# Queries, keys and values of a two-layer mixer in five chunks of 512 columns instead of seven narrower ones

## The chip, the core and the metric

The kernel runs on one core of one Trainium2 chip. The metric is the time of one execution on the device in microseconds (us); a median over runs is given where there are several.

## What is computed

Two layers, one after the other, on a sequence of 256 rows of 1024 columns. Each layer is, cut to what matters:

```python
h = rms_norm(x, norm_g)                        # 256 x 1024
proj = h @ w_in                                # 1024 x 3584
a_q, a_k, a_v, a_g, b_q, b_k, b_v, b_g, m_q, m_g = split(proj)   # 8 x 384, 2 x 256
qa, ka = rope(rms_norm(heads(a_q))), rope(rms_norm(heads(a_k)))  # 6 heads of 64
oa = attention(qa, ka, a_v, causal)
ob = attention(rope(norm(b_q)), rope(norm(b_k)), b_v, three dilated patterns)  # 6 heads
m_k, m_v = split(rms_norm(mem, mem_norm_g) @ w_mem_kv)           # 256 rows of memory
om = attention(rms_norm(heads(m_q)), rms_norm(heads(m_k)), m_v)  # 4 heads, no mask
y = concat([oa * silu(a_g), ob * silu(b_g), om * silu(m_g)])
x = x + y @ w_out
```

All of it is float32.

## The kernel before

**Tiles and engines.** The 256 rows are two tiles `t` of 128; the 1024 columns of the normed input are eight blocks `k` of 128. A projection to n columns sums eight `k`, for both `t`, into two PSUM banks (`project`, L216); gates are projected transposed (`project_t`, L235). Each float32 weight is loaded into `raw` (three buffers, the DMAs issued by SyncE), cast by ScalarE (ACT) into `hi` (L467), and VectorE (DVE) subtracts to get the rest, `lo` (L468); five `hi` and five `lo` can be alive, each 128x1024 or, of a 384-wide chunk, 128x768. The input is split likewise into `xmh` and `xml`. `products` (L146) then issues, for every `k` and `t`, three matmuls: `xmh` with `hi`, `xml` with `hi`, `xmh` with `lo`.

**Chunks.** The columns of the weights come in the order of L410: the memory's keys and values (`mkv`, 512 wide), its queries (`mq`, 256), its gate (`mg`, 256), then for side b and for side a: queries, keys, values (384 each), gate in two parts; then the output projection (`om`, `ob`, `oa`).

**Heads.** `normed` (L270) takes a chunk from PSUM: ACT squares it, DVE sums the squares of each head (`hss`, L262), scales them (`ms`, L155), multiplies the chunk by the tables of the rotation (`t`, L281 and L285), adds (L294) and multiplies by the heads' scales (L295), which GpSimd (POOL) makes with a power (L156). `pair_of_heads` (L302) transposes queries and keys on TensorE (PE), copies them to `qkT`, issues the scores (S), and starts two `head`s (L363): masked add with minimum on DVE (L376; without a mask a plain maximum, `nm`, L369), exponentials on ACT (L371, L378), a reciprocal of the sums on DVE (`rinv`, L382), two scalings on ACT (L384), then transposes of the probabilities `pr` on PE and a copy to `pT` (L395). The values (V) follow, and `y` (L359) is split into `yT` (L593, L594). `pr` has three buffers (`PR_BUFS`).

**What sets the order.** PE's order is written by a planner: `clock` adds the estimated time of each matmul, `spawn` starts a pair or a head after a delay (`D_NORM`, `D_MEM`, `D_SOFTMAX` and others), `poll` lets waiting ones issue between the `k` steps of a projection, `until` holds one back until its turn. The other engines take their instructions in program order as long as `pinning[0]` holds, that is from the start to the end of the memory's queries in layer 0 and for a few steps later; after that a tile scheduler orders them. Each engine's order is fixed when the kernel is built, and an instruction whose input is late holds what stands behind it on its engine. `split(s)` issues casts and subtractions up to `ahead[0]` units ahead of the weights that PE takes. `normed_rows`, `next_mem` and `row_scale` make the normed input, the next layer's memory and the row scales `rmem` of the memory, whose rows `mem_sb` are loaded late (L503).

Of the kernel before, what the change touches and what calls it, by code (L numbers as in the profile page):

```python
# [27 lines left out]
PR_BUFS = 3  # L28
# [39 lines left out]
def hybrid_kernel(ctx: ExitStack, tc: tile.TileContext, x, mem, mem_t, gains, w_in, w_out, w_mem_kv, qk_g, const, out):  # L68
# [26 lines left out]
    mem_sb = cp.tile([P, NT, D], F32, name="mem_sb")  # L95
# [174 lines left out]
    def normed(accs, n, dsts, tables, scale=None):  # L270

        h = n // HD
        half = dict(s=2, d=HD // 2)
        held = []
        for t, acc in enumerate(accs):
            t2, ss = head_squares(acc, n)
            rs = head_scale(ss, n, 1.0 / HD)
            t1 = sp.tile([P, n], F32, tag="t1", name="t1", bufs=2)
            first = tables[0][t][:, None, :].to_broadcast([P, h, HD])
            if scale is None:  # L280
                pin(nc.vector.tensor_tensor(heads(t1), heads(acc), first, op=ALU.mult))  # L281
            else:
                pin(nc.vector.scalar_tensor_tensor(heads(t1), heads(acc), scale, first, op0=ALU.mult, op1=ALU.mult))
            if len(tables) > 1:
                pin(nc.vector.tensor_tensor(t2.rearrange("p (h s d) -> p h s d", **half),  # L285
                                            acc.rearrange("p (h s d) -> p h s d", **half)[:, :, ::-1, :],
                                            tables[1][t].rearrange("p (s d) -> p s d", s=2)[:, None]
                                            .to_broadcast([P, h, 2, HD // 2]), op=ALU.mult))
            held.append((t1, t2, rs))

        def rest():
            for (t1, t2, rs), dst in zip(held, dsts):
                if len(tables) > 1:
                    pin(nc.vector.tensor_tensor(t1, t1, t2, op=ALU.add))  # L294
                pin(nc.vector.tensor_tensor(heads(dst), heads(t1), rs.unsqueeze(2).to_broadcast([P, h, HD]),  # L295
                                            op=ALU.mult))
# [3 lines left out]
    live = dict(pr=0, pT=0, o=0, heads=0, pairs=0, s=0, t=0, v=0)  # L300

    def pair_of_heads(qn, kn, pair, masks, v, gate, ready, finished, alone):  # L302
# [10 lines left out]
        yield from until(lambda: live["s"] == me and live["pr"] + 2 <= PR_BUFS)  # L313
# [3 lines left out]
        live["pr"] += 2  # L317
        scores = [work() for _ in range(2)]
# [8 lines left out]
        for j in range(2):  # L327
            rest = head(2 * me + j, scores[j], spans, masks, pTs, D_SOFTMAX - 1.5 * alone)
            spawn(rest, next(rest))
        yield D_SOFTMAX - 1.5 * alone  # L330
        yield from until(lambda: len(pTs) == 2)
        yield D_PT - alone
# [65 lines left out]

    in_cols = {}
    for i, name in enumerate(["aq", "ak", "av", "ag", "bq", "bk", "bv", "bg"]):  # L400
        in_cols[name] = (i * 384, 384)
    for side in "ab":
        c = in_cols[side + "g"][0]
        in_cols[side + "g0"], in_cols[side + "g1"] = (c, 256), (c + 256, 128)
    in_cols["mq"] = (3072, 256)
    in_cols["mg"] = (3328, 256)
    e_rows = {"om": (6, 2), "ob": (3, 3), "oa": (0, 3)}
    order = []
    for l in range(DEPTH):
        order += [(l, c) for c in ["mkv", "mq", "mg", "bq", "bk", "bv", "bg0", "bg1", "aq", "ak", "av", "ag0", "ag1", "om", "ob", "oa"]]  # L410
    units = []
    for i, (l, c) in enumerate(order):
# [3 lines left out]
        else:  # L416
            n = 512 if c == "mkv" else in_cols[c][1]
# [8 lines left out]
    def loads():  # L426
        while loaded[0] < len(units):
# [4 lines left out]
            if c == "mkv":  # L432
                src = w_mem_kv[l]
            elif c in in_cols:
                src = w_in[l][:, in_cols[c][0]:in_cols[c][0] + n]
            else:
                src = w_out[l][e_rows[c][0] * P:, :]
# [4 lines left out]
            step = 1 if u == 0 else 2 if u == 1 else 4 if u == 2 else nk  # L442
            for b in range(0, nk, step):
                e = b + step
                queue = nc.scalar if u == 0 and b < 3 else nc.sync
                pin(queue.dma_start(raws[u][:, b:e],
                                    src[(a + b) * P:(a + e) * P, :].rearrange("(k p) n -> p k n", p=P)))
# [54 lines left out]
    load(RAW_BUFS + 1)  # L502
    pin(nc.sync.dma_start(mem_sb, mem.rearrange("(t p) c -> p t c", p=P)))  # L503
# [15 lines left out]
    for l in range(DEPTH):  # L519
# [46 lines left out]
        else:  # L566
            mkv, steps = project(mem_xs, weights(), 512)
# [16 lines left out]
        def head_tiles(n, nv):  # L584
            return [sp.tile([P, NT, n], F32, tag=c, name=c, bufs=1) for c in ("qn", "kn")] + [
                sp.tile([P, NT, nv], F32, tag="v", name="v", bufs=2),
                sp.tile([P, n // P, T], F32, tag="gate", name="gate", bufs=2)]
# [8 lines left out]
        def start_heads(pairs, e0, qn, kn, masks, v, gate, ready, delay=D_NORM):  # L596
            for pair in range(pairs):
                spawn(pair_of_heads(qn, kn, pair, masks, v, gate, ready,
                                    lambda y, e=e0 + pair: finished(y, e), e0 + pair == 2), delay + D_PAIR * pair)


        qn, kn, kv, gate = head_tiles(256, 512)
        v = kv[:, :, 256:512]
        ready = dict(gate=1e9)
        mq, steps = project(xs, weights(), 256)
# [134 lines left out]
```

## Time and profile before

| | |
|---|---|
| median of 3 runs | 289.95 us (289.36 to 290.56) |
| the profiled execution | 289.94 us |
| its span in the trace | 288.1 us |
| PE busy | 282.3 us, 1810 groups of instructions |
| DVE busy | 205.9 us |
| ACT busy | 199.0 us |
| POOL busy | 53.4 us |
| DMA, share of the span | q1: 48.7% of 16 engines, 46.22 MB |

The profile comes from one execution; the time beside its span is that execution's own. The chain of waits follows the work that ended last back to the start; the list of waits names what an engine stood still for; the timeline gives each group of instructions with its start, and with the idle time before it and who ended that.

### The profile page before, as it was taken

How to read it: one execution, taken by the hardware profiler on the slowest of the kernel's cores; microseconds unless marked ns; L12 is line 12 of the kernel's file. 1: busy time of each engine (PE TensorE's matmuls, PEld its weight loads, DVE VectorE, ACT ScalarE, POOL GpSimd, SP SyncE). 2: the span in 40 equal slices, each digit the busy share in tenths (PEclk: the TensorE clock that was granted, in tenths of full speed). 3: DMA queues.
4: the chain of work that ended last, by engine and by line, in shares of the span. 5: the costliest groups of instructions: out<-in, count | busy, mean ns of one | idle time of the engine just before them, and what ended most of it. 6: DMA issues, size and time to landing. Idle time of an engine off the chain costs nothing.

```text
span 288.1 us, 4967 instructions
## 1 busy us (share of the span) xinstructions
PE 282.3 (98%) x1810; PEld 250.5 (87%) x1810; DVE 205.9 (71%) x461; ACT 199.0 (69%) x446; POOL 53.4 (19%) x72
## 2 busy tenths in 40 slices
PE   6999999999999999999999999999999999999994
PEld 5799999898989998777788999989898989897773
DVE  1798999794659987754686576979755899655423
ACT  3899678877678779688267554868685778777620
POOL 0103993200003300000020079403000312000000
PEclk9999999999999999999999999999999999999999
DMA  7999675527430656528024918360845443820003
GB/s 246 390 367 369 207 220 161 170 55 273 111 109 17 206 171 262 190 109 290 1 91 168 275 54 236 131 175 9 281 115 154 146 132 96 361 73 0 3 0 146
DMA packets 32793, 47.33 MB, mean 164 GB/s; under 512 B 1280, under 2 KB 27648, under 8 KB 32768
## 3 DMA queue, kind: packets, MB, share of 16 engines
q1 hardware_dynamic: 32336, 46.22, 48.7%
q10 hardware_dynamic: 432, 0.79, 0.9%
q8 instruction: 14, 0.23, 0.3%
q14 instruction: 11, 0.09, 0.1%
HBM read 45.96 MB, written 1.05 MB: 163 GB/s over the span
## 4 chain that ended last, share of the span: by engine, by line
PE 97%; DMA 1%; DVE 0%; SPq 0%; DVEq 0%; issue 0%
PE acc L111 79%; PE wk L114 8%; PE wk L111 5%; PE o L111 5%; DMA memT<-in_mem_t_dram 1%; PE o L114 0%; DVE x_sb L706 0%; SPq L487 0%; DVE whole L533 0%; DVEq L736 0%; DVEq L533 0%
## 5 line engine op out<-in xcount | busy, mean ns | idle before, releaser
L468 DVE TENSOR_TENSOR lo<-raw,hi 128x768 fp32r<-128x768 f32 (+1 forms) x90 | 95.3, 1087 | 20.4 <-ACT hi L467 19.3
L467 ACT CAST hi<-raw 128x768 fp32r<-128x768 f32 (+1 forms) x90 | 82.5, 937 | 26.8 <-PE acc L111 16.9
L111 PE MATMUL acc<-hi,xmh 128*128 128x384 f32 (+2 forms) x252 | 66.6, 346 | 0.0
L111 PE MATMUL acc<-lo,xmh 128*128 128x384 f32 (+2 forms) x252 | 63.7, 335 | 0.0
L111 PE MATMUL acc<-hi,xml 128*128 128x384 f32 (+2 forms) x252 | 63.6, 334 | 0.0
L156 POOL TENSOR_TENSOR hrs<-ms,mhalf 128x6 f32<-128x6 f32 (+1 forms) x24 | 29.9, 1248 | 116.0 <-DVE ms L155 115.7
L111 PEld LDWEIGHTS acc<-hi,xmh 128*128 128x128 f32 x252 | 43.0, 189 | 4.1 <-issue 2.2
L111 PEld LDWEIGHTS acc<-lo,xmh 128*128 128x128 f32 x252 | 45.0, 188 | 1.1
L111 PEld LDWEIGHTS acc<-hi,xml 128*128 128x128 f32 x252 | 44.9, 188 | 1.1
L111 PE MATMUL acc<-hi,yT 128*128 128x512 f32 x128 | 40.9, 401 | 0.0
L111 PE MATMUL acc<-xmh,hi 128*128 128x256 f32 x128 | 29.7, 293 | 0.0
L378 ACT ACTIVATE pr<-pr,nm 128x128 f32<-128x128 f32 (+1 forms) x48 | 21.3, 445 | 12.0 <-DVE nm L376 12.0
L111 PE MATMUL acc<-xmh,lo 128*128 128x256 f32 x128 | 28.4, 283 | 0.0
L111 PE MATMUL acc<-xml,hi 128*128 128x256 f32 x128 | 28.3, 283 | 0.0
L111 PEld LDWEIGHTS acc<-hi,yT 128*128 128x128 f32 x128 | 23.0, 188 | 4.8 <-issue 0.7
L384 ACT ACTIVATE pr<-pr,rinv 128x128 f32<-128x128 f32 (+1 forms) x64 | 25.5, 461 | 0.0
L111 PE MATMUL acc<-lo,yT 128*128 128x512 f32 x64 | 25.1, 391 | 0.0
L111 PEld LDWEIGHTS acc<-xml,hi 128*128 128x128 f32 x128 | 21.0, 191 | 0.0
L111 PEld LDWEIGHTS acc<-xmh,lo 128*128 128x128 f32 x128 | 21.0, 191 | 0.0
L111 PEld LDWEIGHTS acc<-xmh,hi 128*128 128x128 f32 x128 | 20.9, 191 | 0.0
L376 DVE CUSTOM_DVE_ANT_0 pr<-wk,cst 128x128 f32<-128x128 f32 (+1 forms) x48 | 14.3, 353 | 8.6 <-PE wk L111 8.3
L395 ACT COPY pT<-wk 128x384 f32<-128x384 f32 (+1 forms) x32 | 15.2, 508 | 7.2 <-PE wk L114 7.1
(83 smaller groups left out, 354.6 us busy)
## 6 DMA issues: line engine op xcount, KB each, us to landing
raw<-in_w_in_dram SPq DMA_DIRECT2D x24, 768.0 KB, 5.5
raw<-in_w_in_dram SPq DMA_DIRECT2D x7, 1024.0 KB, 6.6
raw<-in_w_out_dram SPq DMA_DIRECT2D x6, 1024.0 KB, 4.9
raw<-in_w_in_dram SPq DMA_DIRECT2D x6, 512.0 KB, 4.1
raw<-in_w_out_dram SPq DMA_DIRECT2D x4, 512.0 KB, 4.2
raw<-in_w_mem_kv_dram SPq DMA_DIRECT2D x2, 1024.0 KB, 5.7
raw<-in_w_mem_kv_dram SPq DMA_DIRECT2D x2, 512.0 KB, 6.7
x_sb<-in_x_dram SPq DMA_DIRECT2D x2, 512.0 KB, 6.4
```

What stands on the lines that cost most here:

```text
L111: pe(nc.tensor.matmul(out, a, b, start=start, stop=stop), us)
L114: pe(nc.tensor.transpose(out, a, ident), 0.109)
L156: pin(nc.gpsimd.tensor_tensor(dst, ms, mhalf[:, :n], op=ALU.pow))
L376: nc.vector.tensor_tensor_reduce(out=pr[:, spans[t]], in0=s[:, spans[t]], in1=masks[t], scale=-1.0, scalar=3e38, op0=ALU.add, op1=ALU.min, ...
L378: nc.scalar.activation(pr[:, spans[t]], pr[:, spans[t]], AF.Exp, scale=-1.0, bias=nm[:, t:t + 1], accum_out=sums[:, t:t + 1])
L384: nc.scalar.activation(pr[:, spans[t]], pr[:, spans[t]], AF.Copy, scale=rinv[:, t:t + 1])
L395: nc.scalar.copy(pT[:, :n], ps[:, :n])
L467: pin(nc.scalar.copy(hi, raw))
L468: pin(nc.vector.tensor_tensor(lo, raw, hi.bitcast(F32), op=ALU.subtract))
```

## The change

The six 384-wide chunks of queries, keys and values and the memory's 256-wide queries become five of 512: `c0` = `mq` and columns 128 to 384 of `bv`; `c1` = `bq` and the first 128 of `bk`; `c2` = the rest of `bk`, the first 128 of `aq`, the first 128 of `bv`; `c3` = the rest of `aq` and 256 of `ak`; `c4` = the rest of `ak` and `av`. Gates, `mkv` and output stay. A chunk that joins several column ranges has a DMA for each. `normed` takes spans of columns with their tables and several destinations. Queries and keys of one side share a tile `qk`, and the pairs start as their columns are complete: b's pair 0 after `c1`, its pairs 1 and 2 after `c2`; a's pairs 0 and 1 after `c3`, its pair 2 after `c4`. The values of `bv` that come with `c0` are copied before `c0`'s norm. The memory's row scales, key norm and gains move from behind the memory's queries into the steps of `c0`; `mem_sb` takes the place of the first weights' buffer. `pr` has four buffers; the memory's pairs start 6.5 instead of 9 planner microseconds after the queries; after a 512-wide norm the delay is 9.5; the delays of the partner, of the scores and of two pairs' softmax change.

```diff
-PR_BUFS = 3
+PR_BUFS = 4
...
-D_NORM, D_MEM, D_QK, D_SOFTMAX, D_PT, D_EVAC = 8, 1, 2.5, 5, 2.5, 4
+D_NORM, D_WIDE, D_MEM, D_QK, D_SOFTMAX, D_PT, D_EVAC = 8, 9.5, 6.5, 2.5, 5, 2.5, 4
...
-D_PARTNER, D_SCORES = 5, 14
+D_BUSY, D_SCORED = 1.5, 4
+D_PARTNER, D_SCORES = 8, 14
...
-    mem_sb = cp.tile([P, NT, D], F32, name="mem_sb")
...
+            for a, b, tables in spans:
+                h = (b - a) // HD
+                first = tables[0][t][:, None, :].to_broadcast([P, h, HD])
...
+                for a, b, dsts in outs:
+                    pin(nc.vector.tensor_tensor(
+                        heads(dsts[t]), heads(t1[:, a:b]),
+                        rs[:, a // HD:b // HD].unsqueeze(2).to_broadcast([P, (b - a) // HD, HD]), op=ALU.mult))
...
-        yield from until(lambda: live["s"] == me and live["pr"] + 2 <= PR_BUFS)
+        yield from until(lambda: live["s"] == me and live["pr"] + 2 <= PR_BUFS and clock[0] >= live["next"])
...
+    for name, pieces in (("c0", (("mq", 0, 256), ("bv", 128, 384))), ("mg", (("mg", 0, 256),)),
+                         ("c1", (("bq", 0, 512),)), ("c2", (("bk", 128, 384), ("aq", 0, 128), ("bv", 0, 128))),
+                         ("bg0", (("bg", 0, 256),)), ("bg1", (("bg", 256, 384),)),
+                         ("c3", (("aq", 128, 640),)), ("c4", (("ak", 256, 768),)),
...
-        order += [(l, c) for c in ["mkv", "mq", "mg", "bq", "bk", "bv", "bg0", "bg1", "aq", "ak", "av", "ag0", "ag1", "om", "ob", "oa"]]
+        order += [(l, c) for c in ["mkv", "c0", "mg", "c1", "c2", "bg0", "bg1", "c3", "c4", "ag0", "ag1", "om", "ob", "oa"]]
...
+    mem_sb = sp.tile([P, NT, D], F32, tag="yT0", name="mem_sb", bufs=1)
     pin(nc.sync.dma_start(mem_sb, mem.rearrange("(t p) c -> p t c", p=P)))
...
         else:
+            ahead[0] = SPLIT_BUFS - 2
             mkv, steps = project(mem_xs, weights(), 512)
...
+            if i == 1 and l == 0:
...
+                r_mem += [row_scale(mem_sb, t, "rmem", mem_junk) for t in range(NT)]
+                sums = [head_squares(k, 256)[1] for k in keys]
...
             if i == 3 and l == 0:
-                mem_junk = sp.tile([P, D], F32, tag="v", name="mem_junk", bufs=2)
-                r_mem.append(row_scale(mem_sb, 0, "rmem", mem_junk))
...
-                split(at[1] + t + 3)
...
+        for t, acc in enumerate(accs):
+            pin(nc.scalar.copy(v_b[:, t, 128:384], acc[:, 256:512]))
...
-        start_heads(2, 6, qn, kn, None, v, gate, ready, D_NORM + D_MEM)
+        start_heads(range(2), 6, qn, kn, None, v, gate, ready, D_MEM)
...
-            for i, dst in ((0, qn), (1, kn)):
-                accs = run(project(xs, weights(), 384))
...
+        accs = run(project(xs, weights(), 512))
+        normed(accs, 512, [span(0, 384, 2), span(384, 512, 3)], [(0, 512, by_tile(qk, 0, 512))])()
+        start_heads(range(1), 3, qn, kn, masks, v, gate, ready, D_WIDE)
+        accs = run(project(xs, weights(), 512))
+        normed([acc[:, 0:384] for acc in accs], 384, [span(0, 256, 3), span(256, 384, 0)],
+               [(0, 256, by_tile(qk, 512, 768)), (256, 384, by_tile(qk_a, 0, 128))])()
...
+        start_heads(range(1, 3), 3, qn, kn, masks, v, gate, ready)
```

Two places show how the order moves. The first is DVE in layer 0 around the memory's gate, whose two `lo` are `lo_268` and `lo_305` in before. Before:

```order
L468 TENSOR_TENSOR lo_268<-raw_118,hi_267 128x1024
L155 TENSOR_SCALAR ms_301<-ss_298 128x1
L468 TENSOR_TENSOR lo_305<-raw_118,hi_304 128x1024
L262 TENSOR_REDUCE hss_334<-sq_332 128x4
L155 TENSOR_SCALAR ms_337<-hss_334 128x4
```

After, where `lo_347` and `lo_363` are the gate's, `lo_321` is the last of `c0`, and the rows of `v_260` are the memory's keys:

```order
L262 TENSOR_REDUCE hss_306<-sq_304 128x4
L642 TENSOR_SCALAR r2_308<-rmem_290 128x1
L155 TENSOR_SCALAR ms_311<-hss_302,r2_308 128x4
L642 TENSOR_SCALAR r2_314<-rmem_296 128x1
L155 TENSOR_SCALAR ms_317<-hss_306,r2_314 128x4
L480 TENSOR_TENSOR lo_321<-raw_117,hi_320 128x1024
L649 SCALAR_TENSOR_TENSOR t1_338<-v_260,rmem_290,gB_94 128x256
L652 TENSOR_TENSOR v_260<-t1_338,hrs_310 128x256
L649 SCALAR_TENSOR_TENSOR t1_341<-v_260,rmem_296,gB_94 128x256
L652 TENSOR_TENSOR v_260<-t1_341,hrs_316 128x256
L480 TENSOR_TENSOR lo_347<-raw_267,hi_346 128x1024
L480 TENSOR_TENSOR lo_363<-raw_267,hi_362 128x1024
```

The gate's first `lo` moved from ahead of the memory's key norm to behind it.

The second place is b's pair 0 in layer 0: DVE from the last work ahead of its two softmaxes (`pr_909` and `pr_920` in before) to the first reciprocal. Before:

```order
L468 TENSOR_TENSOR lo_864<-raw_832,hi_863 128x768
L468 TENSOR_TENSOR lo_939<-raw_832,hi_938 128x768
L376 ISA pr_909,nm_910<-wk_898,cst_94 128x128
L376 ISA nm_910 128x1
L376 ISA pr_909,nm_910<-wk_898,cst_94 128x256
L376 ISA nm_910 128x1
L376 ISA pr_920,nm_921<-wk_899,cst_94 128x128
L376 ISA nm_921 128x1
L376 ISA pr_920,nm_921<-wk_899,cst_94 128x256
L376 ISA nm_921 128x1
L468 TENSOR_TENSOR lo_980<-raw_861,hi_979 128x768
L382 RECIPROCAL rinv_916<-sums_911 128x2
```

After, where the rows of `qk` are the last of `c2`'s norm:

```order
L301 TENSOR_TENSOR qk_498<-t1_802,hrs_798 128x128
L384 ISA pr_846,nm_847<-wk_835,cst_93 128x128
L384 ISA nm_847 128x1
L384 ISA pr_846,nm_847<-wk_835,cst_93 128x256
L384 ISA nm_847 128x1
L384 ISA pr_857,nm_858<-wk_836,cst_93 128x128
L384 ISA nm_858 128x1
L384 ISA pr_857,nm_858<-wk_836,cst_93 128x256
L384 ISA nm_858 128x1
L367 SCALAR_TENSOR_TENSOR y_880<-o_841,gate_261 128x256
L480 TENSOR_TENSOR lo_922<-raw_817,hi_921 128x1024
L390 RECIPROCAL rinv_853<-sums_848 128x2
```

The masked adds stand behind a norm instead of behind subtractions, and `y` of the memory's second pair now stands between them and the reciprocal.

PE at the same place, from the scores of b's pair 0. Before, the transposes of `pr` come 45 gate matmuls and one group of transposes later:

```order
L111 MATMUL acc<-xmh,lo 128x256 x2
L111 MATMUL wk<-qkT 128x128 x2
L111 MATMUL wk<-qkT 128x256 x2
L111 MATMUL o<-pT,v 64x256 x4
L114 MATMUL wk<-ident,qn 128x128
```

After, the rows just ahead of the transposes of `pr`, which also come 45 gate matmuls behind the values:

```order
L111 MATMUL acc<-xmh,hi 128x256
L111 MATMUL acc<-xml,hi 128x256
L111 MATMUL acc<-xmh,lo 128x256
L114 MATMUL wk<-ident,qk 128x128 x4
L114 MATMUL wk<-ident,pr 128x128 x3
```

The queries' and keys' transposes moved from right behind the values to right ahead of the transposes of `pr`; the distance from scores to these stayed.

## Rows read from the trace of the kernel before

**Rows 1.** The page: engines' busy time; the last chain's share by engine

```profile
PE 282.3 (98%) x1810; PEld 250.5 (87%) x1810; DVE 205.9 (71%) x461; ACT 199.0 (69%) x446; POOL 53.4 (19%) x72
...
PE 97%; DMA 1%; DVE 0%; SPq 0%; DVEq 0%; issue 0%
```

**Rows 2.** The list of waits of PE: us in total, times, longest

```profile
PE acc L111 <- DVE whole L533: 1.1, 1, 1.1
PE warm L121 <- DVE mhalf L84: 1.0, 1, 1.0
```

**Rows 3.** Timeline of PE: start, us, engine, line, operation, tiles, count

```profile
12.72 1.07 PE L111 MATMUL acc<-hi,xml 128*128 128x512 f32 x4
13.63 1.07 PE L111 MATMUL acc<-lo,xmh 128*128 128x512 f32 x4
...
19.02 0.40 PE L111 MATMUL acc<-hi,xmh 128*128 128x256 f32 x2
...
30.92 0.51 PE L111 MATMUL acc<-hi,xml 128*128 128x384 f32 x2
...
35.43 0.51 PE L111 MATMUL acc<-lo,xmh 128*128 128x384 f32 x2
```

**Rows 4.** The chain of waits, 30 to 80 us: start, us, what

```profile
39.97 1.06 PE wk L111 x8
41.03 6.46 PE acc L111 x36
...
65.89 0.86 PE wk L111 x8
66.75 1.01 PE o L111 x8
67.77 0.59 PE wk L114 x4
68.35 5.39 PE acc L111 x45
73.74 0.33 PE wk L114 x3
```

**Rows 5.** Timeline of ACT, layer 0, the memory's rows and the memory's squares

```profile
23.07 1.06 ACT L161 ACTIVATE mem_junk<-mem_sb 128x1024 f32<-128x1024 f32 x1 [0.40 <-DMA mem_sb<-in_mem_dram]
24.04 0.18 ACT L161 ACTIVATION_READ_ACCUMULATOR mem_junk<-mem_sb 128x1 f32 x1
...
25.06 0.65 ACT L260 ACTIVATE sq<-acc 128x256 f32<-128x256 f32 x2
```

**Rows 6.** Timeline of DVE: the memory's key norm, and two 1024-wide subtractions

```profile
28.11 0.73 DVE L262 TENSOR_REDUCE hss<-sq 128x4 f32<-128x256 f32 x2
28.76 0.20 DVE L624 TENSOR_SCALAR r<-rmem 128x1 f32<-128x1 f32 x1
...
32.36 0.47 DVE L632 SCALAR_TENSOR_TENSOR t<-v,rmem,gB 128x256 f32<-128x256 f32 x1
...
33.67 0.55 DVE L635 TENSOR_TENSOR kn<-t,hrs 128x256 f32<-128x256 f32 x1
...
155.03 2.36 DVE L468 TENSOR_TENSOR lo<-raw,hi 128x1024 fp32r<-128x1024 f32 x2 [0.63 <-ACT hi L467]
```

**Rows 7.** Timeline of ACT: copies, exponentials and scalings of the memory's pairs

```profile
47.97 1.07 ACT L395 COPY pT<-wk 128x512 f32<-128x512 f32 x2
...
51.24 0.47 ACT L371 ACTIVATE pr<-wk,nm 128x256 f32<-128x256 f32 x1 [2.19 <-DVE nm L369]
...
52.60 0.91 ACT L384 ACTIVATE pr<-pr,rinv 128x256 f32<-128x256 f32 x2
```

**Rows 8.** Timeline of DVE: maxima, norm of 384 columns, first masked add

```profile
50.51 1.29 DVE L369 TENSOR_REDUCE nm<-wk 128x2 f32<-128x512 f32 x2
...
57.31 1.02 DVE L294 TENSOR_TENSOR t<-t,sq 128x384 f32<-128x384 f32 x2
...
66.78 0.29 DVE L376 CUSTOM_DVE_ANT_0 pr<-wk,cst 128x128 f32<-128x128 f32 x1 [2.04 <-PE wk L111]
```

More of the change, by code (lines that the diff above doesn't have):

```diff
@@ L297, in normed, with pair_of_heads @@
         return rest
     pending = {}
-    live = dict(pr=0, pT=0, o=0, heads=0, pairs=0, s=0, t=0, v=0)
-    def pair_of_heads(qn, kn, pair, masks, v, gate, ready, finished, alone):
+    live = dict(next=0, pr=0, pT=0, o=0, heads=0, pairs=0, s=0, t=0, v=0)
+    def pair_of_heads(qn, kn, pair, masks, v, gate, ready, finished, alone, busy):
         ps = work()
@@ L317, in pair_of_heads @@
         live["pr"] += 2
+        live["next"] = clock[0] + D_SCORED
         scores = [work() for _ in range(2)]
@@ L416, in hybrid_kernel @@
         else:
-            n = 512 if c == "mkv" else in_cols[c][1]
+            n = 512 if c == "mkv" else sum(hi - lo for lo, hi in in_cols[c])
             nk = 8 if n <= 256 else 4
@@ new lines, in hybrid_kernel @@
+            if i == 1 and l == 0:
+                mem_junk = sp.tile([P, D], F32, tag="tab", name="mem_junk", bufs=1)
+                r_mem += [row_scale(mem_sb, t, "rmem", mem_junk) for t in range(NT)]
+                sums = [head_squares(k, 256)[1] for k in keys]
+                scales = []
+                for t in range(NT):
+                    r2 = sp.tile([P, 1], F32, tag="r2", name="r2", bufs=2)
+                    pin(nc.vector.tensor_scalar(r2, r_mem[t], r_mem[t], 1.0 / HD, op0=ALU.mult, op1=ALU.mult))
+                    scales.append(head_scale(sums[t], 256, r2))
@@ new lines, in hybrid_kernel @@
+            if i == 3 and l == 0:
+                pin(nc.sync.dma_start(cst, const))
+                load_gains(0, 4)
+                for t in range(NT):
+                    t1 = sp.tile([P, 256], F32, tag="t1", name="t1", bufs=2)
+                    pin(nc.vector.scalar_tensor_tensor(heads(t1), heads(keys[t]), r_mem[t],
+                                                       gB[:, l, 5][:, None, :].to_broadcast([P, 4, HD]),
+                                                       op0=ALU.mult, op1=ALU.mult))
+                    pin(nc.vector.tensor_tensor(heads(kn[:, t]), heads(t1),
+                                                scales[t].unsqueeze(2).to_broadcast([P, 4, HD]), op=ALU.mult))
@@ L642, in hybrid_kernel, with span @@
         tab = prepare_tables(l)
+        def span(a, b, kind):
+            return a, b, [[tab[:, kind, c, t] for t in range(NT)] for c in range(2)]
         gates(run(project_t(xs, weights(), 256)), gate)
@@ new lines, in hybrid_kernel @@
+        for t, acc in enumerate(accs):
+            nc.scalar.copy(v[:, t, 0:128], acc[:, 384:512])
+        start_heads(range(1, 3), 3, qn, kn, masks, v, gate, ready)
+        ready["v"] = clock[0] + D_EVAC
+        gates(run(project_t(xs, weights(), 256)), gate[:, 0:2])
+        gates(run(project_t(xs, weights(), 128)), gate[:, 2:3])
+        masks = [cst[:, C_CAUSAL + 128:C_CAUSAL + 256], cst[:, C_CAUSAL:C_CAUSAL + 256]]
+        if l + 1 < DEPTH:
+            mem_xs = xm_tiles()
+            spawn(next_mem(mem_xs, gT[:, 24 + 8 * l:32 + 8 * l]), D_FIRST_MEM)
@@ new lines, in hybrid_kernel @@
+        (v, gate), qk = head_tiles(384, 384), qk_a
+        qn, kn = qk[:, :, 0:384], qk[:, :, 384:768]
+        ready = dict(v=1e9)
+        accs = run(project(xs, weights(), 512))
+        normed(accs, 512, [span(0, 256, 0), span(256, 512, 1)], [(0, 512, by_tile(qk, 128, 640))])()
+        start_heads(range(2), 0, qn, kn, masks, v, gate, ready, D_WIDE)
+        accs = run(project(xs, weights(), 512))
+        normed([acc[:, 0:128] for acc in accs], 128, [span(0, 128, 1)], [(0, 128, by_tile(qk, 640, 768))])()
@@ L671, in hybrid_kernel @@
+        for t, acc in enumerate(accs):
+            nc.scalar.copy(v[:, t], acc[:, 128:512])
+        start_heads(range(2, 3), 0, qn, kn, masks, v, gate, ready)
+        ready["v"] = clock[0] + D_EVAC
+        gates(run(project_t(xs, weights(), 256)), gate[:, 0:2])
+        gates(run(project_t(xs, weights(), 128)), gate[:, 2:3])
         whole_banks = [(t, c, 512) for t in range(NT) for c in (0, 512)]
```

133 lines of the change are left out of this document (51 added, 82 removed), and 1 row of the table in_cols.

## The prediction

> **What bounds the kernel now.** I read the page first, then the chain of waits, then PE's list of waits, then the timelines of the stages that change. PE is busy 282.3 us of a span of 288.1 us, and the chain that ended last is PE for 97% [rows 1]. PE stands still only twice, in the first microseconds [rows 2]: after that it never waits for anyone. So there are two ways to move the time: give PE fewer or cheaper instructions, or make it wait where it does not wait now. The other engines' busy shares, about 70%, say nothing on the second; only the order at each place does. A row's us of DVE or ACT runs about 0.09 beyond the start of the next instruction (1.06 listed, 0.97 from start to start [rows 5]); I take it off in chains.
>
> All sums are made against the profiled execution, 289.94 us, of which 1.84 lie around the span; the median of the runs, 289.95, is the same number. A difference of 0.5%, about 1.45 us, is about what a measurement of this kernel can tell from no change.
>
> **Fewer matmuls: a gain of 2.5.** From start to start, four matmuls of 512 columns take 0.91, which is 0.2275 for one; 26 of 384 take 4.51, 0.1735 for one [rows 3]; 45 of 256 take 5.39, 0.120 for one [rows 4]. At the granted clock of the higher level, 2.4 GHz, the columns alone would be 0.2133, 0.160 and 0.1067: each matmul has 13 to 14 ns on top. A layer's seven chunks had 6 x 48 + 48 = 336 matmuls, five have 240, with the same 2560 columns per k, t and product. That is 192 fewer in two layers. By the pitches a layer falls from 6 x 48 x 0.1735 + 48 x 0.120 = 55.7 to 240 x 0.2275 = 54.6, 2.2 in all; by 13.4 ns each it is 2.6. PE's trains of matmuls are broken eight times more (66 against 58), at most 0.015 each. I take 2.5, between 2.1 and 2.6. All of it lies on the path, since PE is the path.
>
> The Trainium skill ("TensorE: Matmul & The Clock Gate", section "Wait — 56ns, not 53.3ns?") puts the fixed cost of a warm matmul at about 2.5 ns. By it 192 fewer would give 0.5 and not 2.5. The rows speak against it, with five times that, in this form of matmul.
>
> **The memory's gate in layer 0: a loss of 0.9.** The row scales and key norm of the memory now stand ahead of the gate's first `lo` on DVE. PE starts `c0` where it started the queries, at 19.02 [rows 3], takes 48 x 0.227 = 10.9 for it, and wants that `lo` after four matmuls of the gate, at 30.4. The helpers: the memory's rows land at 23.07 [rows 5]; two squares with their sums read out, 1.06 each, to 25.2; two squares of 256, 0.28 each [rows 5], to 25.8; the second sum over heads 0.32 and the hand-over, to 26.3; four small instructions at 0.2 [rows 6], to 27.1; the last `lo` of `c0`, 1.13 (half of 2.36 less the overlap [rows 6]), to 28.25; the key norm's four instructions at 0.38 and 0.46, 1.7 in all [rows 6], to 30.0; the gate's `lo`, 1.2, to 31.2. PE waits 0.8 to 1.0; I take 0.9, with 0.4 and 1.5 as ends, since POOL's powers and the hand-overs can each be a few tenths off. In layer 1 the gate's `lo` is ahead of the key norm, and nothing is late.
>
> `mem_sb` in the slot of the first weights adds a wait on SP for their release; the queue behind it holds the gains and the next weights. Those first weights are the first four k of `mkv`, which PE has left by 12.7 [rows 3], and the rows land ten microseconds later; I cost it at nothing. Would the load start a microsecond later, the chain above would grow by that microsecond.
>
> **Pair 0 of side b: a loss of 2.4 in each layer.** This is the largest term. Let Z be the end of the first memory pair's scores. PE's order to the scores of pair 0 is: 72 matmuls of 512 (rest of `c1`, all of `c2`) 16.3; the second memory pair's scores 1.06 and 0.21 by which the train behind them is longer (36 x 0.1735 = 6.25 against 6.46 [rows 4]); three groups of four transposes at 0.44 and one of eight at 0.88 (0.11 a transpose [rows 4]); a pair's values 1.22 with the same 0.21; twelve gate matmuls 1.44. Sum: Z + 22.5. The masked scores end at Z + 23.3. From there to the transposes of `pr` it takes as long as in before, 73.74 - 66.75 = 7.0 [rows 4]: PE wants `pr` at Z + 30.3.
>
> The helpers, in their order: the maximum and what is left of a subtraction ahead of it, Z + 1.5 (a maximum 0.6 [rows 8]). ACT then has eight exponentials at 0.46, eight scalings at 0.41, a cast of 0.97 and two copies at 0.49 [rows 5, 7], 8.9 in all, and only then squares `c1`, 0.6: DVE starts `c1`'s norm at Z + 11.0. An operation of 256 columns takes 0.32 [rows 6] and of 384 0.465 [rows 8], so 128 take 0.20 and 512 take 0.60 by the same slope. Per row tile the norm is a sum 0.60, two tables of 384 and 128 columns each 0.67, a small one of 0.1, an add 0.60 and a scaling 0.60, twice, 6.4: Z + 17.4. Five subtractions at 1.13, `y` and its rest at 0.34 each: Z + 23.8. `c2`'s norm: sum 0.465, tables of 256 and 128 at 0.52 twice, 0.1, add 0.465, scalings 0.52, twice, 5.1: Z + 28.9. Only now come the masked adds, two of 128 and two of 256, 1.1: Z + 30.0. `y` of the second memory pair 0.34, a subtraction 1.13, the reciprocal 0.2: Z + 31.6. Two scalings on ACT 0.8: Z + 32.4. PE waits 2.1, and 0.35 more at the second head, whose reciprocal stands behind another subtraction: 2.4. PE's and DVE's orders are alike here in both layers, so 4.8.
>
> In before DVE stood idle for 2.04 ahead of the same masked add and started it as soon as the scores were there [rows 8]; the change uses up that slack and some more. No row shows this stretch itself, so both ends: 1.4 if the first maximum is unobstructed (0.9 sooner) and a few joints are shorter; 3.4 if one more subtraction of 1.1 or the narrow pieces of the norms cost more than the slope. As nothing else can be gained there, the end below 1.4 is no wait, a rival.
>
> **Parts at nothing.** The fourth buffer of `pr` lets scores go sooner, not softmax; its cover is the same DVE work. The memory's pairs start after 6.5 instead of 9: the queries' norm ends about 36.1 by the chain of the gate continued, PE comes to their transposes at about 37.4, after its wait; if that cover is gone, it costs the difference one for one. The value copies ahead of `c0`'s norm, two of ACT at about 0.3, lie in the same 1.3. The norms have 14 more small DVE instructions a layer at some 0.06; the widths are the same, and they are inside the terms above. Four casts and subtractions fewer per layer, each wider, leave DVE 0.5 less to do. More DMAs of the same bytes cost SP some issues; the raw buffers they fill are wanted later than PE's time through a chunk. Side a has the same shape but fewer helpers' tasks in front, with 1.5 to spare at least.
>
> **Sum.** 289.94 - 2.5 + 0.9 + 4.8 = 293.1. With both ends of the three terms, 290.7 to 296.1; several ends together are unlikely, so I take 291.0 to 295.4 for this case.
>
> **Rivals.** (1) *The helpers are in time.* If the reciprocal of pair 0 is ready by Z + 29.5, PE never waits there. For it: the chain has some thirty joints, each from a row elsewhere, and 2.1 of 31.6 is 7%. Against it: DVE's list ahead of the masked adds is solid work. The time is 287.4, or 288.3 with the gate's wait. (2) *The waits are half as long*, 2 to 3 in all: 288.7 to 291.0. That is a chain one microsecond shorter in each layer. (3) *The fixed cost of a matmul is small*: the matmuls give 0.4 and the waits stay, 289.94 - 0.4 + 5.7 = 295.2; rows 3 speak against it. (4) *One more wait*, for the second pair of b, whose margin is about 0.4, or for the cast of the last `k` of `c0`, some 0.3: over 295.4.
>
> **Chances.** Forecast 53%, rival 1 20%, rival 2 20%, rival 3 2%, rival 4 5%. The bounds of 0.5% are 288.5 and 291.4. Faster: 20%, rival 1. The same: rival 2 and 3% at the lower edge of the forecast, 23%. Slower: 57%. The range goes from 287.4 to 295.4; about one in ten lies below, where rival 1's gain is larger than its sum, and one in twenty above. The forecast's own range is 291.0 to 295.4.
>
> **What would show it.** Right: matmuls of 512 at 0.227 throughout the five chunks; PE idle once at the gate of the memory in layer 0, released by DVE's `lo`; PE idle twice in each layer ahead of three transposes of `pr`, about 2.1 and 0.35, released by ACT's scaling, which waited for DVE's reciprocal; DVE without a pause from `c1`'s sum over heads to that reciprocal. Wrong: DVE idle ahead of pair 0's masked adds, as in before; a pause of PE at the transposes of queries and keys; a pitch of 512 columns over 0.23.

## The result, and the profile after

The changed kernel takes 296.78 us (median of 4 runs, 295.50 to 297.42) against 290.25 us for the kernel before, measured beside it: a ratio of 1.0228, 95% interval 1.0203 to 1.0253. The sign was forecast, the size was not: 6.5 us more instead of 3.2, and outside the range of 287.4 to 295.4. The profiled execution took 297.31 us, its span is 295.2 us, 7.1 more than before.

The page of the changed kernel, its busy line and its last chain:

```profile
PE 284.7 (96%) x1618; PEld 229.5 (78%) x1618; DVE 206.0 (70%) x477; ACT 198.9 (67%) x438; POOL 55.4 (19%) x72
...
PE 85%; ACT 6%; DMA 5%; DVE 2%; SPq 1%; issue 0%; DVEq 0%; ACTq 0%
```

Against [rows 1], PE has 192 matmuls fewer and is yet busy longer, and the chain leaves PE for 15% of the span. The list of waits of PE (us in total, times, longest) has three entries that [rows 2] did not have:

```profile
PE wk L114 <- ACT pr L392: 3.6, 2, 1.8
PE acc L111 <- DVE lo L480: 1.1, 1, 1.1
PE warm L121 <- DVE mhalf L85: 1.0, 1, 1.0
PE acc L111 <- DVE whole L546: 0.5, 1, 0.5
PE wk L114 <- DVE xn L522: 0.2, 1, 0.2
```

The timeline of PE shows the first two, at the memory's gate in layer 0 and ahead of the transposes of `pr` of side b's pair 0:

```profile
30.56 0.40 PE L111 MATMUL acc<-xml,hi 128*128 128x256 f32 x2
32.09 0.50 PE L111 MATMUL acc<-xmh,lo 128*128 128x256 f32 x2 [1.13 <-DVE lo L480]
...
75.14 0.60 PE L114 MATMUL wk<-ident,qk 128*128 128x128 f32 x4
77.54 0.84 PE L114 MATMUL wk<-ident,pr 128*128 128x128 f32 x3 [1.80 <-ACT pr L392]
...
218.48 0.84 PE L114 MATMUL wk<-ident,pr 128*128 128x128 f32 x3 [1.80 <-ACT pr L392]
```

And DVE and ACT at the second place, in layer 0: the end of `c2`'s norm, the first masked add, the subtraction ahead of the reciprocal, the reciprocal, the scaling:

```profile
73.06 1.15 DVE L301 TENSOR_TENSOR qk<-t,hrs 128x256 f32<-128x256 f32 x4
74.14 0.28 DVE L384 CUSTOM_DVE_ANT_0 pr<-wk,cst 128x128 f32<-128x128 f32 x1
...
75.58 1.21 DVE L480 TENSOR_TENSOR lo<-raw,hi 128x1024 fp32r<-128x1024 f32 x1
76.71 0.15 DVE L390 RECIPROCAL rinv<-sums 128x2 f32<-128x2 f32 x1
...
77.09 0.80 ACT L392 ACTIVATE pr<-pr,rinv 128x128 f32<-128x128 f32 x2
```

The masked adds start right behind the norm, without a pause; the same add had 2.04 of idle time ahead of it in [rows 8]. The scores themselves were done at 68.6.

What nobody had forecast is behind the second pause. The granted clock of TensorE in three stretches of the changed kernel (the stretch, its length, busy time of PE, PEld, DVE, ACT, POOL, then PEclk, share of DMA, GB/s): around the pause of layer 0, around that of layer 1, and the 2.7 us behind the latter.

```profile
75.50:80.50 5.00, 3.13 (x25) 2.51 (x24) 3.54 (x8) 5.00 (x18) 0.00 (x0) 1.00 0.28 78
216.50:221.50 5.00, 3.13 (x19) 2.57 (x18) 3.33 (x7) 4.77 (x16) 0.00 (x0) 0.88 0.33 92
220.50:223.20 2.70, 2.70 (x14) 2.70 (x14) 0.00 (x0) 1.36 (x4) 0.00 (x0) 0.50 1.02 355
```

After the same 1.80 of pause, layer 0 goes on at 2.4 GHz; layer 1 does so at first (its matmuls are 0.12 apart from 219.40 to 219.87) and then falls to 1.2 GHz: the gate's matmuls there are 0.21 apart (220.70 to 220.92 in the timeline) instead of 0.12, and the stretch from the gate to `c3` is 16.06 in layer 1 against 14.69 in layer 0, 1.4 more.

Where the 7.1 of the span went, by the starts of the stages in the two timelines (a plus is time lost):

| place | us |
|---|---|
| start to `c0` (18.96 against 19.02) | -0.1 |
| last cast of `c0` late (`c0` takes 11.37; 48 matmuls at 0.229 with their breaks are 10.99) | +0.4 |
| gate of the memory, layer 0 (7.13 against 5.76) | +1.4 |
| pair 0 of b, pause and the steps around it, 2 x 2.4 | +4.8 |
| lower clock behind it, layer 1 | +1.4 |
| end of the span behind the last matmul | +0.2 |
| the rest: matmuls and small places | -1.0 |

### The profile page after: what moved, and what is told of

Same layout as the page of the kernel before. It is cut to its first block, busy times and chain, and to the rows that moved or that the text cites. A ratio compares the mean times of both kernels' runs of the same rounds, so it can differ in the third digit from the quotient of the medians.

```text
span 295.2 us, 4600 instructions
## 1 busy us (share of the span) xinstructions
PE 284.7 (96%) x1618; PEld 229.5 (78%) x1618; DVE 206.0 (70%) x477; ACT 198.9 (67%) x438; POOL 55.4 (19%) x72
## 3 DMA queue, kind: packets, MB, share of 16 engines
HBM read 45.96 MB, written 1.05 MB: 159 GB/s over the span
## 4 chain that ended last, share of the span: by engine, by line
PE 85%; ACT 6%; DMA 5%; DVE 2%; SPq 1%; issue 0%; DVEq 0%; ACTq 0%
PE acc L111 68%; PE wk L114 7%; PE wk L111 5%; PE o L111 5%; DMA raw<-in_w_in_dram 3%; ACT hi L479 2%; DMA memT<-in_mem_t_dram 2%; ACT pr L386 1%; DVE lo L480 1%; ACT xmh L183 1%; ACT mem_junk L161 1%; ACT pr L392 0%; ACT v L633 0%; SPq L457 0%; DVE v L652 0%
## 5 line engine op out<-in xcount | busy, mean ns | idle before, releaser
L480 DVE TENSOR_TENSOR lo<-raw,hi 128x1024 fp32r<-128x1024 f32 x78 | 94.5, 1227 | 27.5 <-ACT hi L479 27.2
L479 ACT CAST hi<-raw 128x1024 fp32r<-128x1024 f32 x78 | 81.0, 1052 | 36.1 <-PE acc L111 32.3
L111 PE MATMUL acc<-hi,xmh 128*128 128x512 f32 x188 | 61.4, 411 | 0.0
L111 PE MATMUL acc<-hi,xml 128*128 128x512 f32 x188 | 57.7, 392 | 0.0
L111 PE MATMUL acc<-lo,xmh 128*128 128x512 f32 x188 | 57.6, 391 | 0.0
L156 POOL TENSOR_TENSOR hrs<-ms,mhalf 128x4 f32<-128x4 f32 (+3 forms) x24 | 29.9, 1252 | 134.9 <-DVE ms L155 134.1
L111 PEld LDWEIGHTS acc<-lo,xmh 128*128 128x128 f32 x188 | 35.2, 188 | 8.1 <-DVE lo L480 0.3
L111 PEld LDWEIGHTS acc<-hi,xml 128*128 128x128 f32 x188 | 35.3, 188 | 7.9
L111 PEld LDWEIGHTS acc<-hi,xmh 128*128 128x128 f32 x188 | 32.7, 190 | 7.3 <-issue 2.2
L386 ACT ACTIVATE pr<-pr,nm 128x128 f32<-128x128 f32 (+1 forms) x48 | 21.3, 445 | 11.4 <-DVE nm L384 11.2
L111 PE MATMUL acc<-xml,hi 128*128 128x256 f32 x128 | 28.7, 286 | 0.0
L114 PE MATMUL wk<-ident,pr 128*128 128x128 f32 x104 | 17.5, 280 | 3.7 <-ACT pr L392 3.6
```

Of the source, the lines that this page charges most:

```text
L111: pe(nc.tensor.matmul(out, a, b, start=start, stop=stop), us)
L114: pe(nc.tensor.transpose(out, a, ident), 0.109)
L156: pin(nc.gpsimd.tensor_tensor(dst, ms, mhalf[:, :n], op=ALU.pow))
L386: nc.scalar.activation(pr[:, spans[t]], pr[:, spans[t]], AF.Exp, scale=-1.0, bias=nm[:, t:t + 1], accum_out=sums[:, t:t + 1])
L479: pin(nc.scalar.copy(hi, raw))
L480: pin(nc.vector.tensor_tensor(lo, raw, hi.bitcast(F32), op=ALU.subtract))
```

## The experiments

The theory was that DVE's order makes the waits: key norm ahead of the gate's subtraction, `c2`'s norm ahead of the masked adds. The rivals were that the data are late in any order, that a removed wait comes back at the next user, and that the lower clock and the spread between executions have other causes. All edits are to the changed kernel unless said otherwise.

**e_gate: the key norm two steps later.**

```diff
+            if i == 5 and l == 0:
                 for t in range(NT):
                     t1 = sp.tile([P, 256], F32, tag="t1", name="t1", bufs=2)
```

> The changed kernel with one edit: in layer 0 the memory's key norm stands two steps of c0 later, behind the gate's first subtraction on DVE. The scheduler also sets the reciprocal of side b's pair 0 in layer 0 ahead of a subtraction. Theory (DVE's order makes both waits): PE's wait of 1.13 at the gate is gone, the wait ahead of the transposes of pr in layer 0 falls by one subtraction, from 1.80 to about 0.7, layer 1 stays at 1.80; 296.8 - 1.4 - 1.1 = 294.3. Rival (the memory's data are late for any order, PE waits as long for the next user): no more than 0.3 gained at the gate, 295.5 or more.

297.39 us (295.96 to 298.49), ratio 1.0242 (1.0202 to 1.0282): nothing gained in the median. Yet its trace (296.40) has the wait at the gate gone and that of pair 0 in layer 0 too, where 0.7 had been expected to stay; only layer 1's is left. Its list of waits, first and fourth row:

```profile
PE wk L114 <- ACT pr L392: 1.8, 1, 1.8
...
PE wk L111 <- ACT pr L379: 0.3, 1, 0.3
```

Two things took it back in this execution. `c1` and `c2` take 29.79 instead of 28.80: PE, now 1.4 earlier, comes to the memory's second scores before ACT has freed their buffer. And the first eight matmuls took 6.29 instead of 3.86, of which more below. In the two longest executions (298.37 and 298.49) the mean granted clock is 0.988 and 0.987, in the two others 0.993 and 0.994: it was low for about twice as long there, at a place that no trace shows. So the theory holds for both waits, and the rival holds for most of the gain.

**e_first: the masked adds ahead of `c2`'s norm**, in both layers.

```diff
-        normed([acc[:, 0:384] for acc in accs], 384, ...
...
-        start_heads(range(1, 3), 3, qn, kn, masks, v, gate, ready)
+        def second_norm(..., D=2.4 if True else 0):
+            normed(...)
...
+            start_heads(range(1, 3), 3, qn, kn, masks, v, gate, ready, D_NORM - D)
...
+            spawn(second_norm(), 2.4)
```

> The changed kernel with one edit: c2's norm and the pairs that hang on it start 2.4 planner microseconds into the gate, so that the masked adds of side b's pair 0 stand ahead of that norm on DVE, in both layers. Theory (c2's norm ahead of the masked adds is the cause, and the lower clock follows from the pause): both waits of 1.80 with the 0.6 around each go, and the half clock behind the second too; 296.8 - 4.8 - 1.4 = 290.6, mean clock 1.0. Rival 1 (work is conserved: the norm is late instead and PE waits for the transposes of queries and keys): 294 or more, with a new wait released by qk's scaling. Rival 2 (the clock falls for another reason): waits gone, clock still 0.994, 292.

291.34 us (290.61 to 291.62, 10 runs), ratio 1.0034 (1.0019 to 1.0049). 5.4 of the 6.5 are gone, 0.7 less than expected. Of its waits only the start's and the gate's are left:

```profile
PE acc L111 <- DVE lo L480: 1.1, 1, 1.1
...
PE acc L111 <- DVE whole L546: 0.5, 1, 0.5
```

On DVE the masked adds now follow `c2`'s first sum, 1.6 after PE's scores started, and the reciprocal is there five microseconds earlier than PE wants `pr` (76.10):

```profile
69.85 0.27 DVE L384 CUSTOM_DVE_ANT_0 pr<-wk,cst 128x128 f32<-128x128 f32 x1
...
71.18 0.17 DVE L390 RECIPROCAL rinv<-sums 128x2 f32<-128x2 f32 x1
```

On PE the edit also moves the queries' and keys' transposes behind those of `pr`; PE asks for `pr` 7.9 behind the start of the scores, in the changed kernel 7.8, so this is not what saves the wait. The clock is 1.00 in both layers, and its mean is 0.999 or 1.0 in all ten executions. The norm, which ends 1.4 later, makes nobody wait: the slack was on its side all the time.

**e_first_l1: the same edit in layer 1 alone.**

```diff
-        spawn(second_norm(), 2.4)
+        if l == 1:
+            spawn(second_norm(), 2.4)
+        else:
+            next(second_norm(), None)
```

These lines are against e_first.

> The changed kernel with the masked adds first in layer 1 alone; layer 0 keeps its waits at the gate and at pair 0. Theory: layer 1 gains its 2.4 and the 1.45 at the lower clock, 296.8 - 3.9 = 292.9 with clock 1.0. Rival (the lower clock is not from the pause in layer 1): 294.4, clock below 1.0 after one of layer 0's waits.

293.69 us (293.25 to 294.73), ratio 1.0126 (1.0108 to 1.0145). Its trace (293.47, span 291.3) is 3.9 shorter than the changed kernel's, as expected: 2.4 of waiting and 1.4 of clock belong to layer 1. The medians lie 3.1 apart, since two of the changed kernel's four executions had no fall of the clock (see after_b). Layer 0 keeps its pause of 1.80 and its clock, as the stretch of 75.5 to 80.5 shows:

```profile
75.50:80.50 5.00, 3.13 (x25) 2.50 (x24) 3.48 (x8) 5.00 (x19) 0.00 (x0) 1.00 0.29 89
```

**e_late: PE asks for pair 0's `pr` later**, and DVE still takes `c2`'s norm ahead of the masked adds.

```diff
-    ..., e0 + pair in (5, 7)), delay + D_PAIR * i)
+    ..., (e0 + pair in (5, 7)) + 2 * (e0 + pair == 3)), delay + D_PAIR * i)
```

The number counts units of `D_BUSY`, 1.5.

> The changed kernel with one edit: the transposes of pr of side b's pair 0 are issued 3 planner microseconds later, PE doing other matmuls meanwhile; the DVE's order of norm and softmax stays. Theory (PE only asks too early): the waits of 1.80 are gone in both layers, and the low clock with them, 290.6 to 291.5. Rival (what stands behind pr is then late in turn, values and the next pair's buffers): a new wait of 1 to 2 for a later step of the pairs, 293 or more.

298.69 us (298.03 to 300.26), ratio 1.0297 (1.0262 to 1.0333). The waits of 1.80 are gone, but now the gates and the end of the pairs are late, and PE waits for them eight times, most of it in the output projection:

```profile
PE acc L111 <- DVE gate L596: 2.5, 4, 0.9
PE acc L111 <- ACT yT L610: 2.3, 4, 1.0
```

The rival holds: the pairs are a chain of turns, and what one loses, the last ones pay.

**e_both, and again as e_both_b: both edits of order.**

> Both edits together. Theory: no wait of PE over 0.3 after the start, 296.8 - 1.4 - 4.8 - 1.4 = 289.2, that is 1.0 below before: of the 1.6 that the matmuls' pitch by the trace of after is worth (288 x 0.1736 + 48 x 0.1197 - 240 x 0.229 = 0.78 a layer), 0.5 is lost at the last cast of c0 and other small places. Rival (the five chunks cost something else beside the waits, such as more breaks): 290.5 or more. By the prediction's term of 2.5 for the matmuls it would be 288.2.

> The kernel with both edits once more. Its runs had 290.8 to 294.3 without a wait of PE in the trace of a 291.0 run. Theory (it has another pause in its longer runs, from a load or a helper that is late by chance): the trace shows at 292 or more a wait that the first trace lacks. Rival (only the first matmuls' clock): no wait, the first eight longer by the difference.

292.03 us (290.76 to 294.28, 10 runs), ratio 1.0067 (1.0040 to 1.0095): no better than e_first, 2.8 more than expected, so the rival holds, and up to 295.06 in e_both_b. In the first trace (290.95) PE waits for nobody after the start, but the memory's second scores, a group of eight, take 1.88 in the timeline instead of some 1.1:

```profile
47.40 1.88 PE L111 MATMUL wk<-qkT 64*128 64x256 f32 x8
```

In the second trace (295.06) the same scores stand for 3.12, a wait that the first lacks, as expected. The timelines of PE, ACT and DVE there:

```profile
50.85 1.13 PE L111 MATMUL wk<-qkT 64*128 64x256 f32 x6 [3.12 <-ACT pr L379]
...
46.84 1.04 ACT L479 CAST hi<-raw 128x1024 fp32r<-128x1024 f32 x1 [4.50 <-DMA raw<-in_w_in_dram]
...
47.92 1.23 DVE L480 TENSOR_TENSOR lo<-raw,hi 128x1024 fp32r<-128x1024 f32 x1 [3.32 <-ACT hi L479]
49.06 1.28 DVE L377 TENSOR_REDUCE nm<-wk 128x2 f32<-128x512 f32 x2
```

They are read from the bottom: the maximum of the first scores stands behind a subtraction, that behind a cast, and the cast waits for a load of `c2`, which comes in three pieces; the last landed at 46.74 instead of the first trace's 44.04. A late piece of a load holds, through the orders of ACT and DVE, a softmax that has nothing to do with it. The clock is at 0.57 from 51.5 to 55.5 behind this pause too:

```profile
51.50:55.50 4.00, 4.00 (x15) 2.99 (x13) 2.65 (x5) 4.00 (x14) 0.00 (x0) 0.57 0.00 0
```

**e_piece: `c2` from one range of columns**, otherwise e_both. It computes `bk`'s rest and 256 columns of `bv` in place of `aq`'s and `bv`'s first 128.

```diff
-("c2", (("bk", 128, 384), ("aq", 0, 128), ("bv", 0, 128)))
+("c2", (("bk", 128, 640),))
```

> Both edits, and c2 reads 512 neighbouring columns of the weights in one DMA for each half instead of three; so it computes bk's rest and 256 columns of bv in place of aq's and bv's first 128, and the result is not the reference's. The orders of PE, DVE and ACT are those of both edits alone. Theory (the pieces make the load late): the load of c2's second half lands within 4.5 of its issue in every run, the times lie within 1 of each other around 290.8, no wait at the memory's second scores over 0.3. Rival (the load's lateness has nothing to do with its pieces): the spread stays, 290.8 to 295.

291.16 us (290.61 to 291.52, 12 runs), ratio 1.0020 (1.0001 to 1.0039). The spread is 0.9, where e_both has 3.5 in 10 runs and more with e_both_b, and e_mem8 (below, loads in three pieces) 2.7 in 12: with PE's, DVE's and ACT's order unchanged, the pieces are the likely cause of the long executions, though only one trace shows a late one. Two parts of the expectation failed: the load took 5.0 from issue to landing in its trace, not 4.5, and the wait at the memory's second scores stays, 0.36.

**e_scored, e_warm: e_both with the memory's second scores later; and, in e_warm, two more matmuls on blanks at the start.**

```diff
-        live["next"] = clock[0] + D_SCORED
+        live["next"] = clock[0] + D_SCORED + (masks is None)
...
-WARM = 7
+WARM = 9
```

> Both edits (key norm later, masked adds first) and a third: the scores of the memory's second pair one planner microsecond later, since with the gate's wait gone PE stood 0.29 at them for ACT's exponentials and their group took 2.0 instead of 1.4. Theory: that 0.75 in layer 0 comes back, matmul work from the first cast weights to the end is 274.4 (275.1 with both edits), and the median is 0.7 below that of both edits, 291.3. Rival (the buffer of the scores was not the cause): the first scores' successor waits as long, 292.0.

> The same with nine instead of seven matmuls on blanks at the start, which fill the 0.9 that PE stands still before its first weights. Theory (the spread between executions of the changed kernels is the moment at which PE's clock reaches the higher level, with 1 to 6 of the first eight matmuls at 0.853 instead of 0.429): all eight at 0.429, PE reaches the first cast weights at about 8.2 to 8.7, and the median falls by 1 to 2 against e_scored, to 289.5. Rival (the moment has nothing to do with the pause): same spread, no change.

292.34 us (292.06 to 292.55) and 291.85 us (291.81 to 292.64), ratios 1.0075 (1.0062 to 1.0087) and 1.0067 (1.0053 to 1.0080). The scores no longer wait, the transposes of the probabilities do instead (also 0.78 in layer 1):

```profile
49.70 0.66 PE L114 MATMUL wk<-ident,pr 128*128 128x128 f32 x4 [0.50 <-ACT pr L379]
...
51.91 0.66 PE L114 MATMUL wk<-ident,pr 128*128 128x128 f32 x4 [0.18 <-ACT pT L403]
```

So it is ACT's exponentials, not the buffer of the scores, that are behind there, and the 0.7 expected did not come. e_warm has the same waits but one; its 0.5 less is a wait of 1.05 for a copy of values that its trace lacks, not the start: the first cast weights come at 8.38 there and at 8.20 in e_scored. Its theory fails.

**before_warm: ten matmuls on blanks in the kernel before.**

```diff
-WARM = 7
+WARM = 10
```

> The kernel before with ten instead of seven matmuls on blanks, which fill its pause of 1.57. Its first eight already run at 0.429 from the first. Theory: nothing to gain, 290.0 within 0.2. Rival (the pause costs in some executions): up to 0.5 less and a smaller spread.

290.13 us, ratio 0.9999 (0.9990 to 1.0008). Nothing, as expected.

**e_mem8: e_both with the memory's pairs 1.5 later.**

```diff
-D_NORM, D_WIDE, D_MEM, ... = 8, 9.5, 6.5, ...
+D_NORM, D_WIDE, D_MEM, ... = 8, 9.5, 8, ...
```

> Both edits, and the memory's pairs start 8 instead of 6.5 planner microseconds after c0; loads in three pieces as in the changed kernel. Theory (the early pairs put the memory's maxima behind a subtraction whose load is late): with 1.5 more the second scores wait for nobody in most executions, 290.2 with a spread under 1.5. Rival (the pairs' work is then late for what follows, c1's norm and pair 0): new waits of PE behind it, 291 or more.

291.90 us (290.98 to 293.68), ratio 1.0048 (1.0025 to 1.0070): the rival holds. The second scores wait no more; the transposes behind them do, in its profiled execution for 1.00:

```profile
54.09 0.66 PE L114 MATMUL wk<-ident,pr 128*128 128x128 f32 x4 [1.00 <-ACT pr L379]
```

**e_pr3: three buffers of probabilities.**

```diff
-PR_BUFS = 4
+PR_BUFS = 3
```

> The changed kernel with three buffers of probabilities. By the prediction, the fourth buffer is worth nothing: the waits at the gate and at pair 0 stay as they are, 296.8 within 1. Rival (the fourth buffer lets the memory's second scores go ahead and so brings the masked adds forward): PE's order moves, and the wait at pair 0 grows by about 2 or moves to the scores.

One execution, 299.45 us: 2.7 above the median of the changed kernel, 1.4 to 1.7 above the two executions beside it (after_b, after_c), in which the clock fell and here it did not (mean 0.999). PE's order changes, and the waits with it; the pauses of 1.80 are gone, others stand in their place:

```profile
PE wk L114 <- ACT pr L392: 2.2, 4, 1.1
PE acc L111 <- ACT yT L610: 1.9, 2, 1.0
```

As far as one execution shows, the fourth buffer was not worth nothing: the planner issues a pair's scores only with two buffers of `pr` free, so with three the pairs' turns move.

**after_b, after_c: the changed kernel again, for its trace.**

> The changed kernel once more, for its trace. What is asked: where its 1.5 to 1.9 between executions lie. Theory (the pause at pair 0 lets the clock fall or not, from one execution to the next): the waits are the same 1.80, 1.80 and 1.1; in a run near 297.3 the matmuls behind one of the pauses take 0.213 for 256 columns for some 3 us, in one near 295.5 they take 0.120 throughout. Rival (the spread lies in the first matmuls, 0.853 or 0.429): the place behind the pauses is alike in all, and the first eight differ.

> As the run before it, a second trace: by the theory a run near 297.3 shows the low clock behind a pause and one near 295.5 does not; by the rival the first eight matmuls differ by as much.

297.71 and 298.02 us. Both have the same waits (1.8 twice, 1.1 to 1.2), and in both the clock is low behind layer 1's pause and not behind layer 0's. The short executions (295.50, 296.26) have no trace, but the mean granted clock of every execution is known: 0.998 in these two, 0.994 in those of 297.31 and 297.42, 0.994 and 0.993 here. A stretch of 2.7 at half clock takes 0.005 off the mean, so the short ones had none, and their spans of 293.4 and 293.5 against 294.8 and 295.2 differ by its price. The theory holds: the same pauses bring the low clock in one execution and not in the next.

## Why the prediction was wrong, point by point

The forecast was 3.2 more, the traces show 7.1. Of the 3.9 between them the lower clock is 1.4, the gain from fewer matmuls (1.0 in the table with small places, not 2.5) 1.5, the gate 0.5, the late cast of `c0` 0.4. The largest term, pair 0, was right.

**PE as the bound, and the second way to move the time: right.** PE waits where it did not, at the two places named (and 0.2 for `xn` at the start).

**Pair 0 of side b: right.** Forecast were a pause of 2.1 and 0.35 more. With Z = 45.0 (the first matmul behind the first memory scores), PE wanted `pr` at Z + 30.6 and got it at Z + 32.5, against 30.3 and 32.4 forecast; the reciprocal started at Z + 31.7 and was forecast to be ready at 31.6. The steps between agree too, so this is not a sum of errors that cancel: `c1`'s norm starts at Z + 11.2 (11.0 forecast), `c2`'s at 23.9 (23.8), the masked adds at 29.1 (28.9). The pause of 1.80 with its restart is 2.4 a layer; the second pause of 0.35 does not show as one, that time lies in the restart. e_first takes it away by order alone. Rivals 1 and 2 are refuted by the trace.

**The fall of the clock behind a pause: not in the prediction at all**, 1.4. This is the step that failed: each pause was priced at its length and the restart, and the matmuls behind it at the higher clock throughout; [rows 2] have no pause of PE after the first microseconds from which its price could be read. Four traces with the pause of layer 1 (after, after_b, after_c, e_gate) show 1.2 GHz behind it, and none of the four with layer 0's pause of the same length (after, after_b, after_c, e_first_l1) shows it there. Nor is the place a rule: by their mean clocks two executions of the changed kernel had no fall at all, and the longest of e_first_l1 (294.73, mean 0.994 against 1.0 in the others) had one although layer 1's pause is gone. With both long pauses gone (e_first) there was none in ten. So a pause may cost almost twice its length; which one does could not be told from the rows.

**Fewer matmuls: mis-sized.** 2.5 was forecast, from a pitch of 0.2275 read off four matmuls in an unbroken train [rows 3]. The chain of waits of the changed kernel gives whole trains between breaks of 6, 18 and 24 matmuls of 512:

```profile
51.11 1.40 PE acc L111 x6
...
52.95 4.13 PE acc L111 x18
...
59.12 5.49 PE acc L111 x24
```

At 0.2275 a matmul they would be 1.365, 4.095 and 5.46: each train has 0.03 to 0.04 on top, whatever its length. The chain of before has 384 wide ones the same way:

```profile
48.37 1.05 PE acc L111 x6
...
57.99 4.17 PE acc L111 x24
```

At 0.1735 they would be 1.04 and 4.16: a break of these costs 0.01. So the pitch was right inside a train, and the price of breaks was not: I had priced only the eight more of them, at 0.015, where every break that was there already becomes dearer by some 0.025 with the wider train. The pitches give 1.1 a layer; some fifteen trains of 512 in the five chunks of a layer take 0.4 of it; 0.7 is left, some 1.4 in all, which fits the -1.0 of the table with the small places in it. The sum over layer 1 of e_piece, where PE waits for nobody, agrees: from start to start the matmuls of `mkv`, the chunks and the gates take 91.9 there and 92.6 in before. So my 2.5 was too high, and rival 3 with its 0.4 too low. The estimate of 0.5 from the figure of the Trainium skill ("TensorE: Matmul & The Clock Gate", section "Wait — 56ns, not 53.3ns?") lies below what the runs show as well.

**The gate of the memory: right in place, 1.4 instead of 0.9.** The wait is 1.13, and the matmuls around it lose 0.25. The gate's subtraction started at 30.81, where 30.0 was forecast. Half of this comes from a step that the chain left out: ACT still copied the memory's keys and values from PSUM when the memory's rows were there (23.04), and squared these from 23.49, not from 23.07. Most of the rest is in the key norm: its two scalings, one behind each of its products, started only at 29.34 and 30.27.

```profile
22.52 1.12 ACT L633 ACTIVATE v<-acc 128x512 f32<-128x512 f32 x2
23.49 1.10 ACT L161 ACTIVATE mem_junk<-mem_sb 128x1024 f32<-128x1024 f32 x1
...
29.34 0.42 DVE L652 TENSOR_TENSOR v<-t,hrs 128x256 f32<-128x256 f32 x1
29.68 0.48 DVE L649 SCALAR_TENSOR_TENSOR t<-v,rmem,gB 128x256 f32<-128x256 f32 x1
30.27 0.43 DVE L652 TENSOR_TENSOR v<-t,hrs 128x256 f32<-128x256 f32 x1
30.81 2.36 DVE L480 TENSOR_TENSOR lo<-raw,hi 128x1024 fp32r<-128x1024 f32 x2
```

In addition `c0`'s last cast was late by 0.4, which stood in rival 4 with a margin of 0.3. The measured time lies where rival 4 put it, above 295.4, but this wait is the smaller part of the way there.

**Parts at nothing: two were not.** The fourth buffer matters (e_pr3), and a late piece of a load costs up to 3.1 once the wait at the gate ahead of it is gone (e_both_b). `mem_sb` landed at 23.04 as in before, and the small DVE steps cost nothing that the traces show. The cover of the memory's pairs was larger than said: the queries' norm ended at 37.1, and PE came to their transposes at 40.2, not at 37.4.

**Two slips in its sums change nothing.** The low ends of the three terms give 290.5, not 290.7, and the slope gives 0.18 for 128 columns, not 0.20; the trace of the changed kernel has 0.20 and, for 512, 0.60.

**What was not reached: a version faster than before.** With both waits removed and one load for `c2` the five chunks still take 1.0020 (1.0001 to 1.0039) of the time before. They gain some 1.4 in matmuls and lose it in layer 0 at `c0`'s last cast (0.4) and at the memory's second scores (2.1 from start to start instead of 1.1), and in both layers at the start of the outputs, which take 29.2 and 29.1 instead of 28.5 and 28.7, in part for a group of transposes that stood ahead of them before.

## What to carry to other kernels

A wider chunk makes one engine's train cheaper and moves the work of the others into larger blocks: look in the order of each helper for a small, urgent step (a mask, a reciprocal) that now stands behind a large one that can wait, and move the large one. Read a pitch from whole trains with their breaks, not from the best stretch. Where an engine that waited never did before, price the pause higher than its length, and a removed wait lower, since the next late helper takes part of it.

## What the runs showed of the hardware

The granted clock fell to its half behind some pauses of PE of 1.80 (layer 1) and behind one of 3.12, for about 3 us, and not behind others of 1.80 at a place with the same instructions (layer 0). The same kernel with the same pauses had the fall in some executions (mean clock 0.994) and not in others (0.998).

The first eight matmuls of the trace, in plain float32, 128x512 (four in the program, each listed twice), were 0.429 apart in before from the second on, and 0.853 for a part of them in others: two of eight in before_warm, four in e_both, six in e_gate. The clock column says 1.00 in these stretches, but the trace's records of the granted clock begin only later, with 1.00, at 7.08 in before_warm, 8.70 in e_both and 10.14 in e_gate, and the distance halves at these very moments; in before they begin at 4.94, ahead of the first of the eight. So the column knows nothing of the time before, and twice the distance says the lower of the two levels. This moves the start of the rest by up to 2.5 in a single execution (first cast weights at 8.16 in the changed kernel, 10.63 in e_gate). More blanks ahead did not end it; what sets the moment of the rise is open.
